# Hybrid decoder layer on one Trainium2 core: the gate and up weights of the SwiGLU as an explicit stream

## The chip, the core and the metric

The kernel runs on one core of one Trainium2 chip. The metric is the device time of one launch in microseconds (us); lower is better. The engines are TensorE (PE, with its weight loads as PEld), VectorE (DVE), ScalarE (ACT), GpSimd (POOL) and SyncE (SP), which issues the DMAs.

## What is computed

One decoder layer on 1,088 tokens (1,024 prompt tokens and 8 x 8 sample tokens): RMSNorm, one input projection, GLA heads and dilated softmax heads, an output projection, then the feed-forward part and a last RMSNorm. The change touches the feed-forward part and what stands next to it:

```python
# D_MODEL = 1024, D_FF = 2816, all float32
h = x + mix                                   # mix = concat(heads) @ w_out
hn = rmsnorm(h, g_ffn)
y = h + (jax.nn.silu(hn @ w_fg) * (hn @ w_fu)) @ w_fd
...
y_prompt = rmsnorm(yp, g_final)
y_sample = rmsnorm(ys, g_final)
```

## The kernel before

Float32 products are made of three matmuls each: every operand is split into `hi` (an ACT copy, L172) and `lo` (a DVE subtraction, L173), and `hi*hi`, `hi*lo` and `lo*hi` are summed in PSUM. `split` is that helper; its two instructions have the lines L172 and L173 whichever tile they serve (`whi`/`wlo` for gate and up weights, `wdhi`/`wdlo` for down's, `ghi`/`glo` for the activated block, `xhi`/`xlo` for the tokens).

The feed-forward part takes the tokens in two halves of 544 (`hf` 0 and 1), and the 2,816 inner features in 11 pairs of 128-wide blocks: 22 calls of `gate_up` in all, numbered 0 to 21 here. A call makes gate and up of its two blocks by the seven products of a Strassen-Winograd scheme (`ORDER`: M1, M6, M5, M7, M2, M3, M4), each 24 matmuls of 272 columns, into PSUM banks `a`, `b` (two of them) and `c`. Each product needs one 128x1024 weight block: A11, A12 and A22 as loaded, S1 to S4 as sums of blocks. POOL makes the four sums (L1095). Blocks and sums take the rooms of a ring of seven (`raw`, 512 KB each). After the products, `after` (L1186 to L1192) combines them into a block `B`: PSUM adds `u`, `v`, `s` on DVE, Silu on ACT, the multiplication on POOL or DVE. `plain` splits `B` into `ghi` and `glo`, and in the next call `down` multiplies that by two blocks of w_down: 8 row tiles `k` with 12 matmuls each into banks a, b, c, b (`ps_d`), each added to the residual `h` by DVE (L1240). A call therefore holds 7 x 24 + 8 x 12 = 264 matmuls.

A scheduler sets the order on each engine by readiness and priority. Loads and sums of a call have a priority offset of 700, the splits of weight blocks 350; nothing else ties them to a place:

```python
with tc.high_priority(offset=700):
    parts = blocks(src, w)
...
with tc.high_priority(offset=350):
    hi, lo = (view(part) for part in parts(block))
```

`load_down` brings two blocks of w_down through two rooms of the same ring `raw`. `final_rows` (called five times in call 11, the first of the second half) finishes the first half's rows in a tile `y` whose tag `wraw` has one room, and sends them out; `h[1]`, 2 MB, is loaded there too. Before the loops, `out_half` makes the output projection of each half: for the second half each of the 16 row tiles is also squared on ACT (L1050 and L1053) and summed on POOL (L1054). `factors(1)` turns that sum into the RMSNorm factors; before, it stands in call 0. `norm_half(1)` uses them in call 10.

Of the kernel before, what the change touches and what calls it, by code (L numbers as in the profile page):

```python
# [11 lines left out]
F32 = mybir.dt.float32  # L12
# [91 lines left out]
def hymba_layer(  # L104
# [926 lines left out]
    def out_half(hf):  # L1031
        os = [load_rows(2 * NH * hf + NH * n) for n in range(2)]
        sq_acc = (ffp if hf else outp).tile([P, 2 * NH], F32, name=f"acc{hf}")
        for f in range(KT):
            if f % 2 == 0:
                ws = load_w_out(f, 1)
            for n in range(2):
# [11 lines left out]
                if f == 0:  # L1049
# [34 lines left out]
    def blocks(src, w):  # L1084

        raw = {}
        turn = [0]

        def room(name):
            t = raw[name] = ffp.tile([P, KT * P], F32, tag="raw", name="raw", bufs=7)[:, :w]  # L1090
            return t

        for name, m, k in (("A11", 0, 0), ("A21", 1, 0), ("A22", 1, 1), ("A12", 0, 1)):
            src(room(name), m, k)
        add = lambda out, a, b, op: pool.tensor_tensor(out=out, in0=raw[a], in1=raw[b], op=op)  # L1095
        add(room("S1"), "A21", "A22", ALU.add)
        add(raw["A21"], "A11", "A21", ALU.subtract)
        raw["S3"] = raw["A21"]
        add(room("S2"), "S1", "A11", ALU.subtract)

        def parts(name):
            if name == "S4":
                add(raw["S2"], "A12", "S2", ALU.subtract)
                raw["S4"] = raw["S2"]
            pair = []
            for part in ("whi", "wlo"):
                if wturn[0] % 3 < 2:
# [3 lines left out]
                pair.append(t[:, :w])  # L1111
            wturn[0] += 1
            split(*pair, raw[name])
            return pair

        return parts

    wturn = [0]

    def winograd(src, w, view, x, nk, after):  # L1120
        with tc.high_priority(offset=700):
            parts = blocks(src, w)
        banks = {"a": psum2.tile([P, 2, 512], F32, tag="a", name="ps_a", bufs=1)[:, :, :NH]}
        for name, block, slot, bk, first in ORDER:
            with tc.high_priority(offset=350):
                hi, lo = (view(part) for part in parts(block))
            if bk not in banks:
                banks[bk] = psum2.tile([P, 2, 512], F32, tag=bk, name=f"ps_{bk}", bufs=2 if bk == "b" else 1)[:, :, :NH]
            for s in range(2):
                for k in range(nk):  # L1130
                    xhi, xlo = x(k, slot)
                    one = lambda l, r, i: mm(out=banks[bk][:, s], lhsT=l[:, k, s], rhs=r, start=first and k == 0 and i == 0,  # L1132
                                             stop=k == nk - 1 and i == 2, skip_group_check=not first)
                    one(hi, xhi, 0)
                    one(hi, xlo, 1)
                    one(lo, xhi, 2)
            with tc.high_priority():
                after(name, banks)
# [35 lines left out]
    def gate_up(i, xs):  # L1174
        s1, u2, v5 = temps()
        B = new_block()

        def src(t, m, k):
            cols = slice((2 * i + m) * P, (2 * i + m + 1) * P)
            t = t.rearrange("p (s k c) -> p s k c", s=2, c=P)  # L1180
            for s, wt in enumerate((w_fg, w_fu)):
                dma(out=t[:, s], in_=wt[:, cols].rearrange("(k two p) c -> two p k c", two=2, p=P)[k])

        def made(slot, c, eng):

            act(out=B[:, slot], in_=c[:, 0], func=AF.Silu)  # L1186
            eng.tensor_tensor(out=B[:, slot], in0=B[:, slot], in1=c[:, 1], op=ALU.mult)

        def after(name, ps):
# [3 lines left out]
            elif name == "M6":  # L1193
                add(u2, s1, "b")
            elif name == "M5":
                add(v5, s1, "c")
            elif name == "M7":
                add(v5, v5, "b")
                made(2, v5, pool)
            elif name == "M2":  # L1200
# [73 lines left out]
    for hf in range(2):  # L1274
        for i in range(NF // 2):
# [5 lines left out]
            if hf == 0 and i == NF // 2 - 1:  # L1281
                xs = norm_half(1)
# [105 lines left out]
```

## Time and profile before

| | |
|---|---|
| median of 3 runs | 1657.88 us (1654.70 to 1661.11) |
| the profiled execution: its own time | 1659.34 us |
| its span in the profile | 1657.6 us |
| mean granted clock of TensorE | 0.952 |
| busy, share of the span: PE / DVE / ACT / POOL | 91% / 60% / 36% / 34% |
| feed-forward part within the span | 781.9 to 1657.6 us |

A share is an average over the whole span, in which the projection, the heads and the feed-forward part have different limits. The feed-forward part takes 876 us, and PE is busy 784 us of these; the rows further down take it apart. The name of a row gives line, engine, operation and tiles (out <- in).

### The profile page before, as it was taken

Reading aid. Unit: us, or ns where it says so; the run is one execution under the profiler, and the core shown is the slowest. Engines: PE = TensorE matmul, PEld = TensorE weight load, DVE = VectorE, ACT = ScalarE, POOL = GpSimd, SP = SyncE. Lnnn points to the kernel's source line nnn. Section 1 sums busy time; section 2 is a strip of 40 time slices with the busy share of each in tenths; the row PEclk is TensorE's granted clock in tenths of the full one; section 3 lists DMA queues with packets and bytes.
Section 4 is the critical chain, followed back from the end, with each engine's and each line's share of the span. In section 5 each row is a group of like instructions: output and inputs, shape, how many; then the busy total and the mean of one; then the engine's idle time right before and its main releaser. Section 6 shows DMA issues by size and latency. Waiting matters only on the chain.

```text
span 1657.6 us, 32292 instructions
## 1 busy us (share of the span) xinstructions
PE 1503.7 (91%) x13363; PEld 1349.4 (81%) x13363; DVE 993.9 (60%) x1673; ACT 590.3 (36%) x1014; POOL 556.1 (34%) x419
## 2 busy tenths in 40 slices
PE   7979999999999998986799999999896999999995
PEld 6867777877777756776799999899886999999995
DVE  5495665632333252346876666766885777666665
ACT  3243332153433453233433333333343333333322
POOL 1493332131121000046633444333542433334411
PEclk9988999999999999988799999999997999999997
DMA  4311021263535366575323222222333322332201
GB/s 148 101 68 35 16 72 37 77 184 106 147 93 143 93 206 182 170 229 168 92 86 101 82 77 90 84 82 85 115 109 131 93 90 77 106 98 78 79 24 54
DMA packets 236659, 170.36 MB, mean 103 GB/s; under 512 B 17728, under 2 KB 223968, under 8 KB 236512
## 3 DMA queue, kind: packets, MB, share of 16 engines
q1 hardware_dynamic: 232304, 168.08, 33.9%
q8 instruction: 105, 1.72, 0.4%
q10 hardware_dynamic: 4208, 0.21, 0.2%
q14 instruction: 42, 0.34, 0.1%
HBM read 142.56 MB, written 25.69 MB: 102 GB/s over the span
## 4 chain that ended last, share of the span: by engine, by line
PE 52%; DVE 18%; POOL 11%; DMA 9%; ACT 4%; issue 4%; SPq 1%; POOLq 0%; ACTq 0%; DVEq 0%
POOL raw L1095 8%; PE ps_mm L201 6%; PE ps_mm L203 6%; PE ps_mm L202 6%; DVE wlo L173 6%; PE ps_b L1132 4%; PE ps_c L1132 3%; PE ps_a L1132 3%; PE ps_d L201 3%; PE ps_d L202 3%; PE ps_d L203 3%; ACT whi L172 3%; DVE glo L173 3%; PE ps_S L840 2%; DMA raw<-in_w_ffn_up_dram 2%
## 5 line engine op out<-in xcount | busy, mean ns | idle before, releaser
L1095 POOL TENSOR_TENSOR raw<-raw 128x1024 f32<-128x1024 f32 x88 | 232.8, 2655 | 518.9 <-DVE wlo L173 336.2
L173 DVE TENSOR_TENSOR wlo<-raw,whi 128x1024 fp32r<-128x1024 f32 x154 | 230.8, 1500 | 104.1 <-ACT whi L172 103.9
L201 PE MATMUL ps_d<-ghi,wdhi 128*128 128x272 f32 (+2 forms) x704 | 214.2, 305 | 41.2 <-DVE h L1240 37.0
L172 ACT ACTIVATE whi<-raw 128x1024 fp32r<-128x1024 f32 x154 | 162.9, 1058 | 210.8 <-issue 80.5
L203 PE MATMUL ps_d<-ghi,wdlo 128*128 128x272 f32 (+2 forms) x704 | 211.0, 301 | 0.9 <-DVE wdlo L173 0.9
L202 PE MATMUL ps_d<-glo,wdhi 128*128 128x272 f32 (+2 forms) x704 | 211.7, 301 | 0.0
L201 PE MATMUL ps_mm<-xhi,whi 128*128 128x384 f32 (+1 forms) x576 | 199.3, 346 | 2.0 <-ACT whi L172 1.6
L203 PE MATMUL ps_mm<-xhi,wlo 128*128 128x384 f32 (+1 forms) x576 | 195.0, 340 | 0.6 <-DVE wlo L173 0.6
L202 PE MATMUL ps_mm<-xlo,whi 128*128 128x384 f32 (+1 forms) x576 | 194.9, 339 | 0.2 <-DVE xlo L278 0.2
L201 PEld LDWEIGHTS ps_d<-ghi,wdhi 128*128 128x128 f32 x704 | 141.4, 201 | 46.3 <-DVE h L1240 41.4
L1132 PE MATMUL ps_b<-xhi,whi 128*128 128x272 f32 x528 | 154.8, 293 | 19.3 <-ACT y L1266 11.3
L1132 PE MATMUL ps_b<-xhi,wlo 128*128 128x272 f32 x528 | 154.1, 292 | 0.8 <-DVE wlo L173 0.8
L1132 PE MATMUL ps_b<-xlo,whi 128*128 128x272 f32 x528 | 153.9, 291 | 0.8 <-DVE xlo L173 0.8
L1240 DVE TENSOR_TENSOR h<-h,ps_d 128x544 f32<-128x544 f32 x168 | 115.6, 712 | 51.4 <-PE ps_d L203 51.1
L203 PEld LDWEIGHTS ps_d<-ghi,wdlo 128*128 128x128 f32 x704 | 141.2, 201 | 1.2 <-DVE wdlo L173 1.2
L202 PEld LDWEIGHTS ps_d<-glo,wdhi 128*128 128x128 f32 x704 | 141.8, 201 | 0.0
L201 PEld LDWEIGHTS ps_mm<-xhi,whi 128*128 128x128 f32 x576 | 110.6, 192 | 12.2 <-issue 7.3
L1132 PEld LDWEIGHTS ps_b<-xhi,whi 128*128 128x128 f32 x528 | 100.9, 191 | 20.6 <-ACT y L1266 11.6
L202 PEld LDWEIGHTS ps_mm<-xlo,whi 128*128 128x128 f32 x576 | 110.5, 192 | 6.7 <-issue 5.7
L203 PEld LDWEIGHTS ps_mm<-xhi,wlo 128*128 128x128 f32 x576 | 110.1, 191 | 7.1 <-issue 5.3
L1132 PE MATMUL ps_a<-xhi,whi 128*128 128x272 f32 x352 | 102.8, 292 | 9.7 <-DVE xa L1046 9.2
L1132 PE MATMUL ps_c<-xhi,wlo 128*128 128x272 f32 x352 | 104.3, 296 | 3.4 <-DVE wlo L173 3.3
(362 smaller groups left out, 3463.2 us busy)
## 6 DMA issues: line engine op xcount, KB each, us to landing
raw<-in_w_ffn_gate_dram SPq DMA_DIRECT2D x88, 256.0 KB, 3.6
raw<-in_w_ffn_up_dram SPq DMA_DIRECT2D x88, 256.0 KB, 4.4
raw<-in_w_ffn_down_dram SPq DMA_DIRECT2D x44, 512.0 KB, 3.4
wraw<-in_w_in_dram SPq DMA_DIRECT2D x22, 512.0 KB, 3.7
raw<-in_cache_swa_k_dram SPq DMA_DIRECT2D x32, 256.0 KB, 4.7
raw<-in_cache_swa_v_dram SPq DMA_DIRECT2D x32, 256.0 KB, 3.6
wraw<-in_w_out_dram SPq DMA_DIRECT2D x12, 512.0 KB, 3.8
xa<-x_dram SPq DMA_DIRECT2D x32, 136.0 KB, 2.4
```

The source lines that it names most:

```text
L172: a = by.tensor_copy(out=hi, in_=raw) if by else act(out=hi, in_=raw, func=AF.Copy)
L173: return a, vec.tensor_tensor(out=lo, in0=raw, in1=hi.bitcast(F32), op=ALU.subtract)
L201: mm(out=ps, lhsT=whi[k], rhs=xhi[k], start=first and k == 0, stop=False)
L202: mm(out=ps, lhsT=whi[k], rhs=xlo[k], start=False, stop=False)
L203: mm(out=ps, lhsT=wlo[k], rhs=xhi[k], start=False, stop=last and k == n - 1)
L840: ins = mm(out=out, lhsT=qres[own, qi * P + 32 * r : qi * P + 32 * r + 32], rhs=rhs, start=True, stop=True)
L1095: add = lambda out, a, b, op: pool.tensor_tensor(out=out, in0=raw[a], in1=raw[b], op=op)
L1132: one = lambda l, r, i: mm(out=banks[bk][:, s], lhsT=l[:, k, s], rhs=r, start=first and k == 0 and i == 0, stop=k == nk - 1 and i == 2, sk ...
L1240: vec.tensor_tensor(out=hk, in0=hk, in1=ps, op=ALU.add)
```

## The change

1. `gate_up_weights(i)` replaces `blocks` and the priorities. It has four parts: `load`, `sums(step)`, `parts(behind)` and the list `made` of split pairs. Product j of a call prepares the weight block of product j + 2: its split is queued behind the instruction that combines product j (`after_all` ties the order with `issue_after`). The last two products prepare the first two blocks of the following call. The following call's loads are issued at j = 0, its S1 and S3 are summed at j = 2 and its S2 at j = 3; a call's own S4 is summed at its j = 0.
2. w_down's two blocks come through the tag `wraw` with its one room, and are loaded and split at j = 0 and j = 1 of the next `gate_up`, behind that product's combining instruction. The last pair of each half is loaded and split directly before its `down`.
3. `plain` is called inside `down`, behind the `h` add of k = 5.
4. The second half's squares leave `out_half`. Calls 1 to 4 load two of the eight row tiles each from x_dram (557 KB), square them with one ACT instruction and add them up on POOL (eight operations of 544 columns). `factors(1)` moves from call 0 to call 5.

```diff
@@ out_half
-        sq_acc = (ffp if hf else outp).tile([P, 2 * NH], F32, name=f"acc{hf}")
+        sq_acc = outp.tile([P, 2 * NH], F32, name="acc") if hf == 0 else None
...
-                if f == 0:
+                if hf:
+                    pass
+                elif f == 0:
                     act(out=sq_acc[:, cs], in_=row, func=AF.Square)
@@ blocks and winograd
-    def blocks(src, w):
...
+    def gate_up_weights(i):
...
+        def load():
+            cols = lambda m: slice((2 * i + m) * P, (2 * i + m + 1) * P)
+            for name, m, k in (("A11", 0, 0), ("A21", 1, 0), ("A22", 1, 1), ("A12", 0, 1)):
+                t = room(name).rearrange("p (s k c) -> p s k c", s=2, c=P)
+                for s, wt in enumerate((w_fg, w_fu)):
+                    dma(out=t[:, s], in_=wt[:, cols(m)].rearrange("(k two p) c -> two p k c", two=2, p=P)[k])
...
+        def sums(step):
+            if step == 0:
+                add(room("S1"), "A21", "A22", ALU.add)
+                add(raw["A21"], "A11", "A21", ALU.subtract)
+                raw["S3"] = raw["A21"]
+            elif step == 1:
+                add(room("S2"), "S1", "A11", ALU.subtract)
+            else:
                 add(raw["S2"], "A12", "S2", ALU.subtract)
                 raw["S4"] = raw["S2"]
+
+        def parts(behind):
+            name = ORDER[len(made)][1]
...
+            with after_all(behind), tc.high_priority(offset=60):
+                split(*pair, raw[name])
+            made.append([t.rearrange("p (s k c) -> p k s c", s=2, c=P) for t in pair])
+
+        return load, sums, parts, made
+
+    @contextmanager
+    def after_all(behind):
+        with ExitStack() as stack:
+            for ins in behind:
+                stack.enter_context(tc.issue_after(ins.ins))
+            yield
@@ gate_up
-    def gate_up(i, xs):
+    def gate_up(xs, own, following, wd):
...
+            with tc.high_priority():
+                ins = after(name, banks)
+            if ins is not None:
+                behind = [ins]
+            if j == 0:
+                own[1](2)
+            if j < 2 and wd is not None:
+                wd(j, behind)
+            if following and j == 0:
+                following[0]()
+            if following and j in (2, 3):
+                following[1](j - 2)
+            if j + 2 < len(ORDER):
+                own[2](behind)
+            elif following:
+                following[2](behind)
         return B
@@ load_down
-        for f in (2 * i, 2 * i + 1):
-            with tc.high_priority(offset=350):
-                raw = ffp.tile([P, KT * P], F32, tag="raw", name="raw", bufs=7)
-                dma(out=raw, in_=w_fd[f * P : (f + 1) * P, :])
-                ws.append([bh.tile([P, D], F32R, tag=f"wd{part}", name=f"wd{part}", bufs=3) for part in ("hi", "lo")])
+
+        def load(j, behind):
+            f = 2 * i + j
+            raw = wpool.tile([P, KT, P], F32, tag="wraw", name="wd_raw", bufs=1).rearrange("p k c -> p (k c)")
+            dma(out=raw, in_=w_fd[f * P : (f + 1) * P, :])
+            ws.append([bh.tile([P, D], F32R, tag=f"wd{part}", name=f"wd{part}", bufs=3) for part in ("hi", "lo")])
+            with after_all(behind):
                 split(*ws[-1], raw)
-        return ws
+
+        return ws, load
@@ down
             with tc.high_priority():
-                vec.tensor_tensor(out=hk, in0=hk, in1=ps, op=ALU.add)
+                ins = vec.tensor_tensor(out=hk, in0=hk, in1=ps, op=ALU.add)
+            if then and k == 5:
+                with after_all([ins]):
+                    then()
@@ the calls
+    calls = [(hf, i) for hf in range(2) for i in range(NF // 2)]
+    own = gate_up_weights(0)
+    own[0]()
+    for step in range(2):
+        own[1](step)
+    for _ in range(2):
+        own[2]([])
+    ready, ws, load = [], None, None
+    sums = ffp.tile([P, 2 * NH], F32, name="acc1")
+    for call, (hf, i) in enumerate(calls):
+        following = gate_up_weights(calls[call + 1][1]) if call + 1 < len(calls) else None
+        B = gate_up(xs, own, following, load)
+        own = following
+        if call in (1, 2, 3, 4):
+
+            t = ffp.tile([P, 4, NH], F32, tag="T", name="T", bufs=1).rearrange("p (k n) t -> p k (n t)", k=2)
+            dma(out=t, in_=x_dram[:, 2 * call - 2 : 2 * call, 2 * NH :])
+            act(out=t, in_=t, func=AF.Square)
+            for k in range(2):
+                if call == 1 and k == 0:
+                    pool.tensor_copy(out=sums, in_=t[:, 0])
+                else:
+                    pool.tensor_tensor(out=sums, in0=sums, in1=t[:, k], op=ALU.add)
+        if call == 5:
+            ps = psum2.tile([P, 2, 512], F32, tag="b", name="ps_f", bufs=2)
+            factors(1, sums, psum2.tile([P, 2, 512], F32, tag="b", name="ps_f", bufs=2)[:, 0], [ps[:, 0], ps[:, 1]])
...
+        if ready:
+            down(ws, ready.pop(), h[hf], lambda: ready.append(plain(B)))
+        else:
+            ready.append(plain(B))
+        ws, load = load_down(i)
+        if (hf, i) == (0, NF // 2 - 1):
+            for j in range(2):
+                load(j, [])
+            down(ws, ready.pop(), h[0])
+            load = None
...
+    for j in range(2):
+        load(j, [])
+    whole, wd = ready.pop(), ws
```

The `hi`/`lo` splits, the sums and DVE's adds then stand otherwise. Three places, as they stand in the two programs:

VectorE (DVE) within one call of the first half, before. `v`, `u` and `s` are the PSUM adds that combine M7, M3 and M4; every `wlo` is the second half of a weight split, every `h` an add of a `down` row tile:

```order
L1190 TENSOR_TENSOR v_11756<-v_11756,ps_b 128x544
L173 TENSOR_TENSOR wlo<-raw,whi 128x1024 x2
L1187 TENSOR_TENSOR B<-B,ps_a 128x272
L1190 TENSOR_TENSOR u_11755<-u_11755,ps_c 128x544
L173 TENSOR_TENSOR wlo<-raw,whi 128x1024
L1190 TENSOR_TENSOR s_11754<-s_11754,ps_b 128x544
L173 TENSOR_TENSOR glo<-B,ghi 128x544
L173 TENSOR_TENSOR wlo<-raw,whi 128x1024
L1240 TENSOR_TENSOR h<-h,ps_d 128x544 x3
L173 TENSOR_TENSOR glo<-B,ghi 128x544
L1240 TENSOR_TENSOR h<-h,ps_d 128x544 x5
```

The same stretch of a call after the change, from the split of M3's block on (the split of M4's block is the `wlo` behind `B`, the next two are M1's and M6's of the next call):

```order
L173 TENSOR_TENSOR wlo<-raw,whi 128x1024
L1266 TENSOR_TENSOR h<-h,ps_d 128x544
L173 TENSOR_TENSOR wdlo<-wd_raw,wdhi 128x1024
L1181 TENSOR_TENSOR B<-B,ps_a 128x272
L173 TENSOR_TENSOR wlo<-raw,whi 128x1024
L1184 TENSOR_TENSOR u_11379<-u_11379,ps_c 128x544
L173 TENSOR_TENSOR wlo<-raw,whi 128x1024
L1184 TENSOR_TENSOR s_11378<-s_11378,ps_b 128x544
L173 TENSOR_TENSOR wlo<-raw,whi 128x1024
L1266 TENSOR_TENSOR h<-h,ps_d 128x544
L173 TENSOR_TENSOR wlo<-raw,whi 128x1024
L1266 TENSOR_TENSOR h<-h,ps_d 128x544 x3
```

Before, one `glo` and one `wlo` stood between `s` and the first three `h`; now a single `wlo` stands there, both `glo` come behind the three `h` (the row after the last one shown), and w_down's second split stands right behind M3's weight split.

GpSimd (POOL), a little over one call of the first half, before (`raw` are the sums of weight blocks, `B` the multiplications):

```order
L1095 TENSOR_TENSOR raw<-raw 128x1024
L1187 TENSOR_TENSOR B<-B,v_11026 128x272
L1095 TENSOR_TENSOR raw<-raw 128x1024 x2
L1187 TENSOR_TENSOR B<-B,u_11025 128x272
L1095 TENSOR_TENSOR raw<-raw 128x1024
L1187 TENSOR_TENSOR B<-B,s_11024 128x272
L1095 TENSOR_TENSOR raw<-raw 128x1024
```

The same queue after the change:

```order
L1104 TENSOR_TENSOR raw<-raw 128x1024 x4
L1181 TENSOR_TENSOR B<-B,v_11380 128x272
L1181 TENSOR_TENSOR B<-B,u_11379 128x272
L1181 TENSOR_TENSOR B<-B,s_11378 128x272
L1104 TENSOR_TENSOR raw<-raw 128x1024 x4
```

The four sums were spread over the call with multiplications between them; now all four stand in a row, ahead of the three multiplications.

SyncE (SP) in call 11 and 12, where the first half's finished rows `y` leave (`out_0_dram`) and w_down's blocks are loaded, with the numbers of the buffers, before:

```order
L1293 DMA h_13423<-x_dram_58 128x8x544
L1271 DMA out_0_dram<-y_13338 128x1024
L1271 DMA out_0_dram<-y_13367 128x1024
L1271 DMA out_0_dram<-y_13396 32x1024
L1218 DMA raw_14143<-in_w_ffn_down_dram 128x1024
L1218 DMA raw_14149<-in_w_ffn_down_dram 128x1024
L1182 DMA raw_14159<-in_w_ffn_gate_dram 128x4x128
L1182 DMA raw_14159<-in_w_ffn_up_dram 128x4x128
```

And after the change, from the last `y` on:

```order
L1300 DMA out_0_dram<-y_13385 32x1024
L1242 DMA wd_raw_13445<-in_w_ffn_down_dram 128x1024
L1102 DMA raw_13822<-in_w_ffn_gate_dram 128x4x128
L1102 DMA raw_13822<-in_w_ffn_up_dram 128x4x128
L1242 DMA wd_raw_13493<-in_w_ffn_down_dram 128x1024
L1242 DMA wd_raw_13810<-in_w_ffn_down_dram 128x1024
L1242 DMA wd_raw_13858<-in_w_ffn_down_dram 128x1024
```

Before, w_down's loads went to rooms of the ring. Now the four stand in one room, `wd_raw`, which is the room of `y` too: the first waits until the last `y` has left, and each of the others until the one ahead of it has been split.

## Rows read from the trace of the kernel before

**Rows 1.** Windows: stretch, length, busy of PE PEld DVE ACT POOL, clock, DMA share, GB/s.
```profile
781.88:863.48 81.60, 66.78 (x448) 64.39 (x449) 61.12 (x70) 31.11 (x40) 47.73 (x30) 0.82 0.30 90
863.48:1155.69 292.21, 276.44 (x2114) 274.69 (x2113) 201.04 (x200) 100.03 (x129) 113.22 (x56) 0.96 0.30 87
1155.69:1333.66 177.97, 149.25 (x1099) 145.27 (x1097) 138.82 (x186) 67.19 (x88) 74.30 (x44) 0.93 0.35 109
1333.66:1587.01 253.35, 240.05 (x1850) 238.53 (x1849) 174.76 (x175) 87.52 (x113) 99.45 (x50) 0.97 0.30 88
```

**Rows 2.** The chain of waits within one call: start, duration, engine, tile, line.
```profile
1370.65 3.00 PE ps_a L1132 x24
...
1382.04 2.35 POOL raw L1095
...
1386.12 5.76 POOL raw L1095 x2
...
1391.90 1.07 ACT whi L172
...
1392.99 1.23 DVE wlo L173
1394.22 0.63 DVE s L1190
1394.85 2.43 DVE glo L173
1397.27 1.70 DVE wlo L173
```

**Rows 3.** Waits, 1333 to 1587: who waited for whom, total, times, longest.
```profile
PE ps_d L201 <- DVE h L1240: 13.3, 7, 1.9
```

**Rows 4.** Windows of one call at full clock and one not, then 3.3 us each.
```profile
1370.49:1405.82 35.33, 33.40 (x267) 33.18 (x265) 25.01 (x25) 12.50 (x17) 14.17 (x7) 1.00 0.31 90
1405.82:1442.67 36.85, 34.94 (x266) 34.72 (x265) 25.03 (x25) 12.51 (x17) 14.16 (x7) 0.95 0.29 86
...
1435.96:1439.30 3.34, 3.34 (x17) 3.34 (x17) 2.24 (x4) 0.00 (x0) 0.00 (x0) 0.52 0.32 125
1399.67:1403.00 3.33, 3.33 (x26) 3.33 (x27) 3.10 (x6) 0.00 (x0) 0.00 (x0) 1.00 0.49 157
```

**Rows 5.** Timeline of PE around a short wait.
```profile
1327.90 0.39 PE L201 MATMUL ps_d<-ghi,wdhi 128*128 128x272 f32 x1 [0.45 <-DVE h L1240]
...
1328.26 0.28 PE L203 MATMUL ps_d<-ghi,wdlo 128*128 128x272 f32 x1
```

**Rows 6.** Timeline of DVE in the call of rows 2.
```profile
1387.10 2.50 DVE L173 TENSOR_TENSOR wlo<-raw,whi 128x1024 fp32r<-128x1024 f32 x1 [1.57 <-ACT whi L172]
```

**Rows 7.** The sums on POOL, 1330 to 1590: duration in ns, min/median/max.
```profile
L1095 POOL TENSOR_TENSOR raw<-raw x28: 2385/2397/3392, 1345.2 to 1575.5; 128x1024 f32<-128x1024 f32 x28
```

**Rows 8.** The second half's sums of squares, and who waited for them.
```profile
L1054 POOL TENSOR_TENSOR acc<-acc,sq x28: 757/776/1639, 723.8 to 788.6; 128x272 f32<-128x272 f32 x28
...
PE ps_f L1063: 3.8, 1
```

**Rows 9.** Small DVE operations, 1200 to 1300: duration in ns, min/median/max.
```profile
L156 DVE TENSOR_TENSOR st<-st x15: 151/159/2309, 1221.5 to 1285.8; 128x1 f32<-128x1 f32 x15
```

**Rows 10.** Timeline of SP: the last three issues of `y` to leave, from first to last.
```profile
1257.57 30.51 SPq L1271 DMA_DIRECT2D out_dram<-y  x3
```

**Rows 11.** Timeline of PE and ACT there.
```profile
1289.21 0.59 PE L201 MATMUL ps_d<-ghi,wdhi 128*128 128x272 f32 x1 [3.00 <-DVE st L1258]
...
1275.64 1.02 ACT L1266 ACTIVATE y<-ps_y 32x1024 f32<-32x1024 f32 x1 [0.55 <-DMA out_dram<-y]
```

**Rows 12.** Landing times in us: loads (page, median) and `y` (min/median/max).
```profile
raw<-in_w_ffn_up_dram SPq DMA_DIRECT2D x88, 256.0 KB, 4.4
raw<-in_w_ffn_down_dram SPq DMA_DIRECT2D x44, 512.0 KB, 3.4
...
DMA to landing us min/median/max: 1.9/2.6/9.5
```

More of the change, by code (lines that the diff above doesn't have):

```diff
@@ L1110, in parts @@
                     t = bh.tile([P, KT * P], F32R, tag=part, name=part, bufs=1)
[L1111 to L1124, printed above, removed]
-            with tc.high_priority(offset=350):
[L1126 to L1138, printed above, removed]
+                pair.append(t)
+            turn[0] += 1
+            with after_all(behind), tc.high_priority(offset=60):
[8 more added lines that the diff above has]
+            yield
     def temps():
@@ L1193, in after @@
             elif name == "M6":
[L1194 removed]
+                return add(u2, s1, "b")
             elif name == "M5":
[L1196 removed]
+                return add(v5, s1, "c")
             elif name == "M7":
[L1198 removed]
+                ins = add(v5, v5, "b")
                 made(2, v5, pool)
+                return ins
             elif name == "M2":
[L1201 removed]
+                return made(0, ps["a"], vec)
             elif name == "M3":
[L1203 removed]
+                ins = add(u2, u2, "c")
                 made(3, u2, pool)
+                return ins
             else:
[L1206 removed]
+                ins = add(s1, s1, "b")
                 made(1, s1, pool)
[L1209 to L1210 removed]
+                return ins
+        banks, behind = {}, []
+        n = KT // 2
+        for j, (name, _, slot, bk, first) in enumerate(ORDER):
+            if bk not in banks:
+                banks[bk] = psum2.tile([P, 2, 512], F32, tag=bk, name=f"ps_{bk}", bufs=2 if bk == "b" else 1)[:, :, :NH]
+            hi, lo = own[3][j]
+            for s in range(2):
+                for k in range(n):
+                    xhi, xlo = (part[:, slot] for part in xs[k])
+                    for a, (l, r) in enumerate(((hi, xhi), (hi, xlo), (lo, xhi))):
+                        mm(out=banks[bk][:, s], lhsT=l[:, k, s], rhs=r, start=first and k == 0 and a == 0,
+                           stop=k == n - 1 and a == 2, skip_group_check=not first)
+            with tc.high_priority():
[14 more added lines that the diff above has]
+                following[2](behind)
         return B
@@ L1228, in plain, with down @@
         return hi, lo
-    def down(ws, g, h):
+    def down(ws, g, h, then=None):
         for k in range(KT):
@@ L1244, in hymba_layer @@
     xs = norm_half(0)
[L1245 removed]
+    out_half(1)
     outp.release()
```

61 lines of the change are left out of this document (13 added, 48 removed).

## The prediction, made before the changed kernel ran

> **What bounds the kernel now.** I read the windows first [rows 1]. The feed-forward part falls into a start of two calls (81.60 us), eight regular calls (292.21), four calls around the change of halves (177.97), seven regular calls (253.35) and a tail. A regular call takes (292.21 + 253.35) / 15 = 36.37 us. PE is busy in 94.6% of these stretches and its clock is granted at 0.96 to 0.97, so PE sets their pace, and the question is what its other 5% are. The chain of waits gives the floor: 24 matmuls in 3.00 us [rows 2], 0.125 us each, and 264 x 0.125 = 33.0 us, with edges 33.1. So a call loses 3.3 us.
>
> The waits say where: PE waits once a call, before a row tile of `down`, for an `h` add: 13.3 us in 7 calls, 1.9 each [rows 3]. The windows by call show the other part: 35.33 us at a clock of 1.00, but 36.85 at 0.95 [rows 4]. Two of three calls go like the second. There the stretch behind the wait runs at 0.52, that is at the 1.2 GHz level instead of 2.4, with 17 matmuls in 3.34 us where the other call does 26; that costs 36.85 - 35.33 = 1.5 us. A wait of 0.45 us has no such sequel: the first matmul behind it is slow, two take 0.36 us instead of 0.25 [rows 5].
>
> The chain says why the `h` add is late [rows 2]. POOL makes S1, S3 and S2 late (1382.04, 1386.12), since a room of the ring came free late; S2's and S4's splits slide behind them; `s` ends at 1394.85, and then `glo` (2.43) and `wlo` (1.70) stand in DVE's queue before the first of three `h` adds. PE needs the banks these adds free, and restarts when the first is done.
>
> **The change, part by part.** *Regular calls, removed.* The order rows show that `glo` and its neighbour leave the place between `s` and the three `h`; one `wlo` is left there. 4.1 us of queue become 1.23, so the wait of 1.9 and its sequel of 1.5 go: at most 3.3 us a call.
>
> *Regular calls, added.* POOL's four sums now stand in a row and meet the splits of M3, of w_down and of M4. The chain and the timeline of DVE show what a meeting does [rows 2, 6]: the two sums from 1386.12 take 5.76 us in place of 2 x 2.40 [rows 7], and a `wlo` that starts at 1387.10 takes 2.50 in place of 1.23. The split waited for the sum that was running, went next, and the second sum waited for it. They take turns, whole instruction by whole instruction. The Trainium skill ("SBUF — State Buffer", section "Who interferes with whom") says that a VectorE instruction with two SBUF inputs and a GpSimd instruction that reads SBUF exclude each other, that the one issued first goes, and that the other blocks fully; the rows agree. Were they independent, the sum below would be 11 us lower.
>
> By hand, with 0 at M6's first matmul. PE has M6, M1, M5, M7, M2 and M3, 2 of M4 and 33 of `down` before it needs M4's low part: 179 x 0.125 = 22.4. M6 is done after 48, at 6.0; its add takes 0.63 and M7's `wlo` 1.23, to 7.9. M7's block is S3, made in A21's room, and the ring hands that room to the next call's A22; its up half lands 4.4 later [rows 12], at 12.3. S1 runs to 14.7. M3's `wlo` is queued behind the add of M7 (done at 13.5), so it waits to 14.7 and ends at 15.9 (wanted at 17.0). S3 then runs to 18.3, `wdlo` to 19.5, S2 to 21.9, M4's `wlo` to 23.1. That is 0.7 us late, a short wait like that one [rows 5]. The number of loads is the same but for four, and the DMA engines are 30% busy [rows 1], so their order on SP costs nothing in itself. What else stands in the queues has slack: the multiplications behind the four sums feed `glo`, which is now needed a whole call later. So a call takes 33.1 + 0.6 = 33.7. Bounds: 33.1 (S1 starts outside that second) and 36.4 (the rival below). The gain is 36.37 - 33.7 = 2.7, for the 15 regular calls and for one more in the tail, which begins with the same kind of call: 16 x 2.7 = **-43 us**.
>
> *The start.* The 14 POOL sums of the second half's squares go (0.78 each [rows 8]); one PE wait for them, 3.8 us, goes too. For it, calls 1 to 4 get eight POOL operations of 544 columns. Between 0.78 for 272 and 2.40 for 1024 columns that is some 1.4 us each, an estimate, or 11 us in all, which can hold up a split each time; their four ACT squares and four loads lie beside other work. Bounds -4 and +11; I take **+4**, because the first two calls now also make two calls' splits in a fixed order.
>
> *factors(1) in call 5.* Some 15 small DVE operations enter the queue between the products' adds. Such an operation takes 0.16, but up to 2.31 when a POOL operation holds it up [rows 9]. Eight of them stand ahead of M2's multiplication, which frees bank a: 8 x 0.16 = 1.3 at least, 8 x 2.3 = 18 at most. With ten small PE instructions and one stretch at half clock (1.5) I take **+5**, near the lower end, since the median is 0.16; for the range 0 to +10.
>
> *The change of halves.* The single room `wraw` now serves `y` and all of w_down's loads. Before, the last `y` is issued by 1257.57 + 30.51 = 1288.1 [rows 10], and `down` starts at 1289.21 [rows 11] with weights already there. After: `y` lands 2.6 later, the first load takes 3.4 [rows 12], its split 1.07 + 1.23, the second load and split the same: 1288.1 + 2.6 + 5.7 + 5.7 = 1302.1. PE has 16 matmuls (2.0 us) that need the first block alone, so it waits 12.9 - 2.0 = 10.9, in two pieces. The 1.5 us of half clock behind it stands against a like one before (its wait of 3.00). I take **+11**. Below, 0, if the rows leave earlier than before (the last PE transposes for `y`, 1275.64 on ACT, may come forward); above, +25, if `y` lands in 9.5 [rows 12] and both pieces cost clock.
>
> Sum: -43 + 4 + 5 + 11 = -23 against the profiled execution's own 1659.3, which lies 1.5 above the median of the runs: **1636 us**.
>
> **The rivals.** *A, slower: the turns fall the wrong way.* All hangs on when A22 lands. At 13.4 instead of 12.3, S1 runs to 15.8, M3's `wlo` to 17.0, S3 to 19.4, `wdlo` to 20.6, S2 to 23.0 and M4's `wlo` to 24.2: 1.8 us late. That is as long as the wait removed, so the half clock comes with it: 33.1 + 1.8 + 1.5 = 36.4, nothing gained in any call, and start, factors and boundary are lost: 1659 + 20 = **1679**. It decides from about 1 us of lateness. For it: only one second lies between the cases, and POOL sums of 3.39 occur [rows 7]. Against: landing later than 13.5 lets the split go first, and no wait is left.
>
> *B, no change: the single room and the start cost their upper bounds.* -43 + 11 + 5 + 25 = -2: **1657**; half of that excess gives 1648. For it: the loads of call 12 and call 13 queue in the same room, and landing times of 9.5 stand in the trace. Against: only five `y` tiles pass.
>
> *C, faster: no late split and a cheap boundary.* 16 x 3.3 = -53, start 0, factors +4, boundary +5: **1615**. For it: A22 may land just outside the second. Against: two pieces of it must go well together.
>
> That the change does not do what it says can be left out: the order rows show the splits and sums where the text puts them.
>
> **How the numbers follow.** A run tells no change from change at about 0.5%, 8 us. Likeliest case 0.62 (its own range 1625 to 1648), A 0.11, B 0.14, C 0.13. Faster: 0.62 + 0.13 = 0.75; same: B, 0.14; slower: A, 0.11. The range from 1614 to 1656 takes in C and nearly all of B and leaves A out.
>
> **What would show it.** Right: regular calls of 33.1 to 34.3 us; the 1.9 us wait for `h` gone; a short wait on PE for `wlo` before M4's low part; the granted clock near 1.00 in these windows; around the change of halves a PE wait for `wdlo` or `wdhi` of some 11 us that was not there. Wrong: calls still near 36 with PE waiting for `wlo` (A); regular calls good but the four boundary calls over 195 us (B). If the regular calls are good and the total is still at 1658, the boundary and the start were sized wrong, not the mechanism.

## The result and the profile after

The changed kernel takes 1630.31 us (median of 4 runs, 1627.30 to 1631.03), the kernel before 1656.29 (4 runs). The ratio is 0.9835 with a 95% interval of 0.9809 to 0.9861: 1.65% faster. The span of the profiled execution is 1629.0 us.

The windows of the changed kernel, cut at the same places of the program as those of before [rows 1] and finer (length, busy time of PE, PEld, DVE, ACT and POOL, granted clock, DMA share, GB/s): the two first calls, calls 2 to 4, 5 and 6, 7 to 9, the four calls around the change of halves, the seven regular calls behind it, the tail.

```profile
779.21:858.71 79.50, 67.29 (x454) 64.47 (x455) 56.01 (x53) 34.12 (x41) 54.17 (x31) 0.88 0.41 118
858.71:958.56 99.85, 99.85 (x794) 99.58 (x793) 74.48 (x75) 37.78 (x48) 49.31 (x21) 1.00 0.32 96
958.56:1033.25 74.69, 70.65 (x544) 69.56 (x543) 56.11 (x67) 25.22 (x32) 30.09 (x14) 0.98 0.29 85
1033.25:1133.12 99.87, 99.87 (x795) 99.70 (x794) 74.42 (x75) 37.77 (x48) 49.35 (x21) 1.00 0.33 96
1133.12:1327.91 194.79, 153.43 (x1097) 147.92 (x1096) 137.04 (x186) 68.35 (x87) 74.18 (x44) 0.89 0.32 100
1327.91:1560.86 232.95, 232.95 (x1851) 232.44 (x1850) 173.65 (x175) 88.14 (x112) 115.50 (x50) 1.00 0.30 89
1560.86:1629.00 68.14, 49.07 (x393) 48.42 (x391) 37.36 (x81) 19.16 (x30) 9.36 (x10) 0.87 0.14 49
```

In the regular calls PE is busy for the whole window and its clock is granted at 1.00: 232.95 / 7 = 33.28 us a call. No wait is left in them to remove. Against before, the feed-forward part is 875.7 - 849.8 = 25.9 us shorter, about the change of the median (the two profiled executions differ by 28.6; the rest lies ahead of this part). It is made of -46.3 in 15 regular calls (15 x (36.37 - 33.28)), +8.1 in calls 5 and 6 (74.69 against 2 x 33.28), +16.8 at the change of halves (194.79 against 177.97), -2.1 in the two first calls and -2.5 in the tail.

The wait for `h` of 1.9 us per call [rows 3] is gone; in the list of waits of the seven calls no wait of PE stands at all. How close it is can be read from one call. Timeline of DVE, then POOL, then PE, of the changed kernel (start, duration, line, what is written and read):

```profile
1043.84 0.72 DVE L1184 TENSOR_TENSOR v<-v,ps_b 128x544 f32<-128x544 f32 x1 [1.10 <-PE ps_b L1216]
1044.48 1.89 DVE L173 TENSOR_TENSOR wlo<-raw,whi 128x1024 fp32r<-128x1024 f32 x1
1046.29 0.71 DVE L1266 TENSOR_TENSOR h<-h,ps_d 128x544 f32<-128x544 f32 x1
1046.92 2.81 DVE L173 TENSOR_TENSOR wdlo<-wd_raw,wdhi 128x1024 fp32r<-128x1024 f32 x1
1049.65 0.42 DVE L1181 TENSOR_TENSOR B<-B,ps_a 128x272 f32<-128x272 f32 x1
1050.00 3.06 DVE L173 TENSOR_TENSOR wlo<-raw,whi 128x1024 fp32r<-128x1024 f32 x1
...
1042.88 9.11 POOL L1104 TENSOR_TENSOR raw<-raw 128x1024 f32<-128x1024 f32 x3 [14.23 <-DVE wlo L173]
...
1053.07 0.29 PE L201 MATMUL ps_d<-ghi,wdhi 128*128 128x272 f32 x1
1053.19 0.32 PE L1216 MATMUL ps_b<-xhi,wlo 128*128 128x272 f32 x1
```

Three splits (1.22 us each when alone) take 1.89, 2.81 and 3.06, and three sums (2.40 each) take 9.11 instead of 7.2. M4's split ends at 1050.00 + 3.06 = 1053.06 and PE's first matmul that reads it starts at 1053.19, with no wait in front of it.

What starts this row of sums is not what the prediction names. Before its first sum, S1, POOL waits 14.23 us for a DVE `wlo`. It is the split of M2's block, the last reader of the room that S1 takes. M6's first matmul, the zero of the walk, and the chain on ACT, DVE and SP that leads there:

```profile
1030.73 0.29 PE L1216 MATMUL ps_b<-xhi,whi 128*128 128x272 f32 x1
...
1037.35 0.61 ACT L1186 ACTIVATE s<-ps_a 128x544 f32<-128x544 f32 x1
...
1037.99 0.72 DVE L1184 TENSOR_TENSOR u<-s,ps_b 128x544 f32<-128x544 f32 x1 [6.23 <-ACT s L1186]
1038.62 1.22 DVE L173 TENSOR_TENSOR wlo<-raw,whi 128x1024 fp32r<-128x1024 f32 x1
...
1041.53 1.22 DVE L173 TENSOR_TENSOR wlo<-raw,whi 128x1024 fp32r<-128x1024 f32 x1
...
1026.82 0.51 SPq L1102 DMA_DIRECT2D raw<-in_w_ffn_up_dram  x1
...
1039.92 0.37 SPq L1102 DMA_DIRECT2D raw<-in_w_ffn_gate_dram  x1
```

M7's split is the `wlo` at 1038.62, M2's the one at 1041.53, and S1 starts at 1042.88. By the order of the program's loads, the one at 1026.82 is A22's up half; it lands 3.2 us later, at 1030.03, some 13 us before S1 starts. The load that follows M7's split, at 1039.92, is A12's.

At the change of halves PE now waits for w_down's splits. Timelines of PE and of ACT there, with the idle time ahead of an instruction and what ended it:

```profile
1273.97 0.59 PE L201 MATMUL ps_d<-ghi,wdhi 128*128 128x272 f32 x1 [6.73 <-ACT wdhi L172]
1279.78 0.39 PE L201 MATMUL ps_d<-ghi,wdhi 128*128 128x272 f32 x1 [2.72 <-ACT wdhi L172]
...
1272.86 1.06 ACT L172 ACTIVATE wdhi<-wd_raw 128x1024 fp32r<-128x1024 f32 x1 [1.28 <-DMA wd_raw<-in_w_ffn_down_dram]
1278.67 1.06 ACT L172 ACTIVATE wdhi<-wd_raw 128x1024 fp32r<-128x1024 f32 x1 [4.75 <-DMA wd_raw<-in_w_ffn_down_dram]
```

Before, PE's only wait at this `down` was one of 3.00 for `st` [rows 11].

### The profile page after: what moved, and what is told of

Read it like the earlier page. It is cut to its first block, busy times and chain, and to the rows that moved or that the text cites. A ratio compares the mean times of both kernels' runs of the same rounds, so it can differ in the third digit from the quotient of the medians.

```text
span 1629.0 us, 32149 instructions
## 1 busy us (share of the span) xinstructions
PE 1490.5 (92%) x13363; PEld 1338.2 (82%) x13363; DVE 987.9 (61%) x1673; ACT 590.3 (36%) x1002; POOL 584.1 (36%) x413
## 4 chain that ended last, share of the span: by engine, by line
PE 71%; DVE 12%; DMA 9%; ACT 2%; POOL 2%; issue 2%; SPq 1%; ACTq 0%; DVEq 0%; POOLq 0%
PE ps_b L1216 11%; PE ps_a L1216 6%; PE ps_c L1216 6%; PE ps_mm L201 6%; PE ps_mm L203 6%; PE ps_mm L202 6%; PE ps_d L201 5%; PE ps_d L203 5%; PE ps_d L202 5%; PE ps_S L840 2%; DMA x_dram<-xa 2%; DVE wlo L173 2%; PE ps_X L982 1%; PE ps_T L938 1%; DMA out_dram<-y 1%
## 5 line engine op out<-in xcount | busy, mean ns | idle before, releaser
L1104 POOL TENSOR_TENSOR raw<-raw 128x1024 f32<-128x1024 f32 x88 | 260.1, 2964 | 433.7 <-DVE wlo L173 280.1
L173 DVE TENSOR_TENSOR wlo<-raw,whi 128x1024 fp32r<-128x1024 f32 x154 | 242.2, 1575 | 0.0
L201 PE MATMUL ps_d<-ghi,wdhi 128*128 128x272 f32 (+2 forms) x704 | 205.5, 294 | 16.3 <-ACT wdhi L172 9.4
L202 PE MATMUL ps_d<-glo,wdhi 128*128 128x272 f32 (+2 forms) x704 | 205.6, 293 | 1.1 <-DVE glo L173 1.1
L203 PE MATMUL ps_d<-ghi,wdlo 128*128 128x272 f32 (+2 forms) x704 | 201.2, 292 | 0.0
L1216 PE MATMUL ps_b<-xhi,wlo 128*128 128x272 f32 x528 | 158.1, 299 | 5.6 <-DVE wlo L173 5.6
L201 PEld LDWEIGHTS ps_d<-ghi,wdhi 128*128 128x128 f32 x704 | 135.1, 192 | 18.2 <-ACT wdhi L172 11.6
L202 PEld LDWEIGHTS ps_d<-glo,wdhi 128*128 128x128 f32 x704 | 135.8, 193 | 1.5 <-DVE glo L173 1.5
L203 PEld LDWEIGHTS ps_d<-ghi,wdlo 128*128 128x128 f32 x704 | 133.4, 192 | 0.0
L201 PEld LDWEIGHTS ps_mm<-xhi,whi 128*128 128x128 f32 x576 | 110.7, 192 | 12.2 <-issue 7.3
L1216 PEld LDWEIGHTS ps_b<-xhi,wlo 128*128 128x128 f32 x528 | 103.3, 196 | 7.9 <-DVE wlo L173 6.9
```

The source lines that it names most:

```text
L173: return a, vec.tensor_tensor(out=lo, in0=raw, in1=hi.bitcast(F32), op=ALU.subtract)
L201: mm(out=ps, lhsT=whi[k], rhs=xhi[k], start=first and k == 0, stop=False)
L202: mm(out=ps, lhsT=whi[k], rhs=xlo[k], start=False, stop=False)
L203: mm(out=ps, lhsT=wlo[k], rhs=xhi[k], start=False, stop=last and k == n - 1)
```

## The experiments

All times are medians; the ratio is that to the kernel before, with its 95% interval.

### One line of the change, alone and taken out

e1 is the kernel before with `plain` queued behind k = 5, and nothing else:

```diff
...
-            before, g = g, plain(B)
...
-            if before:
-                down(ws, before, h[hf])
+            if g:
+                made = []
+                down(ws, g, h[hf], lambda: made.append(plain(B)))
+                g = made.pop()
+            else:
+                g = plain(B)
```

> The kernel before with one thing of the change: plain (ghi and glo) is queued behind the h add of k = 5 of down. Sums, splits and rooms stay as before. Theory A (the order of glo in DVE's queue is the whole regular gain): the 1.9 us wait for h falls to 0.9 or less, since only one wlo is left ahead of the first h, the half-clock stretch behind it goes, regular calls take 33.3 to 34.3 us in place of 36.4, and the total is 1610 to 1627. Rival B (the gain comes from POOL's sums starting earlier, which splits and s follow): s and that wlo stay as late as before, a wait of 1 us or more remains, regular calls take 35 us or more, and the total is above 1635.

It takes 1623.30 us, ratio 0.9792 (0.9770 to 0.9814): one change of order, and it is faster than the whole change, by 0.4% with intervals that just touch. Its windows (calls 2 to 9, change of halves, calls 14 to 20):

```profile
858.65:1132.22 273.57, 267.41 (x2115) 265.67 (x2113) 196.06 (x200) 100.06 (x129) 117.24 (x56) 1.00 0.32 93
1132.22:1312.29 180.07, 149.86 (x1098) 145.81 (x1097) 138.40 (x186) 67.77 (x88) 76.53 (x44) 0.92 0.35 108
1312.29:1551.19 238.90, 233.99 (x1850) 232.47 (x1849) 170.62 (x176) 87.56 (x113) 102.97 (x50) 1.00 0.31 93
```

PE's only row among the waits of the last of these (total, times, longest):

```profile
PE ps_d L201 <- DVE h L1247: 4.9, 7, 0.7
```

238.90 / 7 = 34.13 us a call. The wait fell from 1.9 to 0.7 us, and with it the half clock went: the granted clock is 1.00. So 1.2 us of wait and the 1.0 us that the half clock cost on average (1.5 in two of three calls) went together.

e2 is the changed kernel with `plain` ahead of `down` again:

```diff
...
-        if ready:
-            down(ws, ready.pop(), h[hf], lambda: ready.append(plain(B)))
-        else:
-            ready.append(plain(B))
+        ready.append(plain(B))
+        if len(ready) > 1:
+            down(ws, ready.pop(0), h[hf])
```

> The changed kernel without its third part: plain is called before down again, so one glo stands among the h adds of k = 0 to 4 and the other ahead of s. Theory A (glo's place): waits for h of 1 us or more come back in most calls, regular calls take 34.5 us or more, total 1650 or more. Rival B (the earlier sums): with s earlier there is room for glo; regular calls stay at 33.3 to 33.8 us, total 1630 to 1640.

It takes 1631.82 us, ratio 0.9848 (0.9823 to 0.9872), like the changed kernel, and calls 14 to 20 read:

```profile
1326.49:1558.62 232.13, 232.13 (x1851) 232.13 (x1850) 173.24 (x175) 88.48 (x112) 115.98 (x50) 1.00 0.30 89
```

The two runs together say that the wait had two cures, each sufficient for most of it: to queue `plain` later (e1), or to have the rest of the change, with the stream (e2). In e2 one `glo` stands ahead of `s`, as it did not before, and finds DVE idle:

```profile
1448.97 0.73 DVE L173 TENSOR_TENSOR glo<-B,ghi 128x544 fp32r<-128x544 f32 x1 [1.35 <-ACT ghi L172]
1449.61 0.71 DVE L1184 TENSOR_TENSOR s<-s,ps_b 128x544 f32<-128x544 f32 x1
```

So in both runs a single `wlo`, and no `glo`, stands between `s` and the first `h` add; earlier sums with `glo` left in that place were not run. Theory A of e1 held, and so did rival B of e2. The prediction ascribed the gain to `glo` and a neighbour leaving this place, which fits both runs. But the third part of the change, which moves `plain`, is not needed for it: with the stream in place that part is worth nothing.

### Does a split wait for one sum, or for all?

e7 makes S1 twice in each call:

```diff
                 add(room("S1"), "A21", "A22", ALU.add)
+                add(raw["S1"], "A21", "A22", ALU.add)
```

> The changed kernel with the sum S1 made twice in every call, 2.4 us more of POOL ahead of S3 and S2 with the same result; DVE's order stays. Theory A (splits and sums take turns, one sum per split, so that more sums in the row don't make a split later): M4's split ends as before within 0.5 us, regular calls take 33.2 to 33.8 us, total 1628 to 1640. Rival B (a split waits out the sums queued ahead of it): M4's split is 2.4 us or more late, regular calls take 35.5 us or more, total 1665 or more.

It takes 1653.45 us, ratio 0.9974 (0.9954 to 0.9994); seven calls take 240.71 us, 34.39 each. Neither total was right, but the timelines of POOL and DVE tell the theories apart:

```profile
1053.71 5.74 POOL L1104 TENSOR_TENSOR raw<-raw 128x1024 f32<-128x1024 f32 x2 [13.48 <-DVE wlo L173]
1059.40 1.76 POOL L1182 TENSOR_TENSOR B<-B,v 128x272 f32<-128x272 f32 x1
1061.12 6.70 POOL L1104 TENSOR_TENSOR raw<-raw 128x1024 f32<-128x1024 f32 x2
...
1060.80 1.44 DVE L173 TENSOR_TENSOR wlo<-raw,whi 128x1024 fp32r<-128x1024 f32 x1
...
1068.95 1.23 DVE L173 TENSOR_TENSOR wlo<-raw,whi 128x1024 fp32r<-128x1024 f32 x1 [1.25 <-ACT whi L172]
```

M4's split ends at 1062.24, 18.2 us behind M1's start at 1044.08, where the changed kernel has it at 19.8, and PE reads it at 1064.02: it is earlier, not later, although the call holds 2.4 us more of sums. That alone does not decide, since the multiplication of `v` now runs behind the second sum and the split met it, which is shorter, in place of a sum. M3's split decides:

```profile
1055.31 1.87 DVE L173 TENSOR_TENSOR wlo<-raw,whi 128x1024 fp32r<-128x1024 f32 x1
```

It ends at 1057.18, 3.5 us behind the start of S1 at 1053.71. In the changed kernel it ends at 1046.37, also 3.5 behind S1's start, with one sum fewer still queued behind that one. Splits and POOL instructions take turns, one for one; theory A's mechanism holds. What the theory overlooked is the end of the row: S2, now last and later, is the block of the next call's M6, whose split stands in DVE's queue ahead of the first `h` adds (1068.95). So PE waits for `h`, as its waits over two calls say:

```profile
PE ps_d L201 <- DVE h L1267: 1.2, 2, 0.7
```

The length of POOL's row decides over the `h` adds, then, and only its turns over M4's split.

e4 writes the low half of M4's split twice, directly one behind the other:

```diff
-                split(*pair, raw[name])
+                done = split(*pair, raw[name])
+                if name == "A22":
+                    with after_all(done[1:]):
+                        vec.tensor_tensor(out=pair[1], in0=raw[name], in1=pair[0].bitcast(F32), op=ALU.subtract)
```

> The changed kernel with the low half of M4's weight split written twice in every call, one extra DVE instruction of 1.22 us whose result is the same, directly behind the first. In the changed kernel that split ends 0.1 us before PE wants it by the trace. Theory A (the margin is that thin, and this split is the critical one): PE waits for it 1.0 to 1.9 us in every call; if half clock follows, regular calls take 35.8 to 36.7 us and the total is 1670 or more, if not, 34.3 to 35.2 and 1647 to 1662. Rival B (the margin is larger than the trace makes it look): regular calls stay below 33.8 us, total below 1640.

It takes 1645.93 us, ratio 0.9924 (0.9900 to 0.9947); seven calls take 236.92 us, 33.85 each, at a clock of 1.00. This is between the theories, and a reason lies in the edit: the scheduler answered it by placing other matmuls on PE ahead of M4 (24 of `down` where 21 stood), so that 1.2 us more of DVE work met a later need. PE still waits for the second writing in five of the seven calls, 0.2 us at most. So the split is close to PE's need, but how thin the margin of the changed kernel is stays unmeasured.

### The price of the single room

e3 gives w_down's raw blocks a room of their own. The space comes from g_final's row copy, which moves into the factor tile once that is read:

```diff
-            raw = wpool.tile([P, KT, P], F32, tag="wraw", name="wd_raw", bufs=1).rearrange("p k c -> p (k c)")
+            raw = fin.tile([P, KT, P], F32, tag="wdraw", name="wd_raw", bufs=1).rearrange("p k c -> p (k c)")
...
-    gfin = fin.tile([P, D], F32, name="gfin")
-    dma(out=gfin, in_=g_final.partition_broadcast(P))
...
             xs = norm_half(1)
+            gfin = rstd_bc[:, :D]
+            dma(out=gfin, in_=g_final.partition_broadcast(P))
```

> The changed kernel with a room of its own for w_down's raw blocks (g_final's row copy moves into the factor tile, which is free by then). Theory A (the single room is what the change of halves costs): the PE waits for wdhi there, 6.73 and 2.72 us, go with the half-clock stretches behind them; the four calls around the change of halves take 194.8 - 9.5 - 3 = 182 us, the total is 1616 to 1621, regular calls stay at 33.3. Rival B (the loss sits in y's own chain: one room, its way out, the small DVE operations): the waits move to y or st, the four calls stay above 190 us, total 1626 or more.

It takes 1611.69 us, ratio 0.9723 (0.9701 to 0.9745), and the four calls take

```profile
1131.46:1307.04 175.58, 146.72 (x1099) 142.08 (x1098) 136.21 (x186) 68.58 (x87) 80.01 (x44) 0.93 0.36 114
```

175.58 against 194.79: the shared room cost 19.2 us, more than the two PE waits of 9.45 and two stretches at half clock. PE is idle for 28.9 us where it was for 41.4, and busy for 146.7 where it was for 153.4 with the same matmuls, at a clock of 0.93 where it was 0.89. Both waits for `wdhi` are gone. Theory A, with a larger size.

### The price of the fourth part

e5 undoes it:

```diff
...
-                if hf:
-                    pass
-                elif f == 0:
+                if f == 0:
...
-    out_half(1)
+    sums = out_half(1)
...
-        if call in (1, 2, 3, 4):
+        if call in ():
...
-        if call == 5:
+        if call == 0:
```

> The changed kernel without its fourth part: the second half's squares are made in out_half again and factors(1) stands in call 0. Theory A (the squares leaving out_half give the start its gain, and factors in call 5 costs 8.1 us in calls 5 and 6, which take 74.69 in place of 2 x 33.28): calls 5 and 6 fall to 66.6 us, the first matmul of the feed-forward part starts 2 to 3 us later and the two first calls take 2 us more; total 1625 to 1628. Rival B (the start's gain is the stream's): calls 5 and 6 fall and the start keeps its time, total 1621 to 1623.

It takes 1622.86 us, ratio 0.9785 (0.9769 to 0.9802). Calls 5 and 6, and the two first calls' end, read

```profile
856.61:956.48 99.87, 99.87 (x795) 99.59 (x794) 74.48 (x75) 37.77 (x48) 49.34 (x21) 1.00 0.32 96
956.48:1023.06 66.58, 66.58 (x530) 66.40 (x529) 49.68 (x50) 25.18 (x32) 32.91 (x14) 1.00 0.32 96
```

66.58 against 74.69: the price of `factors(1)` in call 5 is 8.1 us. The start gained nothing from moving the squares: its first call begins at 776.25 and call 2 at 856.61, 80.4 us, where the changed kernel has 79.5; in the profiles of all runs here this stretch takes 79.5 to 81.6. The beginning of the feed-forward part itself lies between 775.9 and 781.9 in the profiles with the squares in place, so a difference of 2 or 3 us there is no finding. Rival B.

e6 keeps the squares where the change put them, but queues `factors(1)` behind the last `h` add of call 5:

```diff
...
+            if last and k == KT - 1:
+                with after_all([ins]):
+                    last()
...
+            def second():
+                ps = psum2.tile([P, 2, 512], F32, tag="b", name="ps_f", bufs=2)
+                factors(1, sums, ps[:, 1, 256:], [ps[:, 0], ps[:, 1]])
...
```

> The changed kernel with factors(1) queued behind the last h add of call 5, where DVE is idle for 6.2 us in every call and POOL makes no sum, in one PSUM tile in place of two. Theory A (its small DVE operations cost because they stand among the splits and sums): calls 5 and 6 fall from 74.69 to 67 to 69 us and the total to 1622 to 1625. Rival B (the cost is that of PE's small instructions and of the bank, wherever they stand): 72 us or more, total above 1627.

It takes 1626.92 us (1620.12 to 1628.90), ratio 0.9800 (0.9775 to 0.9825); calls 5 to 7 take 101.86 us, 2.0 over 3 x 33.28. In the trace that is theory A: 8.1 became 2.0, with one PSUM tile in place of two. The total lies between the two theories' ranges. The same small operation in the timeline of the changed kernel:

```profile
970.87 2.24 DVE L154 TENSOR_SCALAR st<-st 128x5 int32<-128x5 int32 x1
```

And in that of e6:

```profile
987.40 0.17 DVE L154 TENSOR_SCALAR st<-st 128x5 int32<-128x5 int32 x1
```

Among the sums it took 2.24 us, where POOL is idle 0.17.

e8 joins the edits of e3 and e6.

> The changed kernel with the room of its own for w_down (1611.7 alone) and with factors(1) at the end of call 5. Theory A (the two losses are independent): 1611.7 less what the other kernel gains, 1603 to 1606. Rival B (the change of halves absorbs part of it): 1607 to 1612.

1609.07 us, ratio 0.9701 (0.9685 to 0.9717): calls 5 to 7 take 101.88, so e6's gain is there, and 2.7 us of it go at the change of halves:

```profile
1125.42:1303.69 178.27, 149.63 (x1098) 144.97 (x1097) 135.99 (x186) 68.73 (x87) 80.08 (x44) 0.91 0.35 112
```

PE is idle there as long as in e3 (28.6 against 28.9 us) but busy 2.9 longer, at a clock of 0.91 against 0.93; why the clock is lower was not followed. The total is in rival B's range.

### A version that beats both

e9 joins the edits of e3 and e5: the stream, the place of `glo`, an own room, and the fourth part undone.

> The changed kernel with a room of its own for w_down and without its fourth part (squares in out_half, factors(1) in call 0): what is left is the stream and the place of glo. Theory A (the two losses add: 19 us at the change of halves, 8 us in calls 5 and 6): 1601 to 1605. Rival B (factors in call 0 takes its price at the start once the rest is faster): 1607 or more.

1607.87 us, ratio 0.9696 (0.9673 to 0.9719). Calls 2 to 9 are at 33.29 us each, but the change of halves takes 181.76. Neither theory's reason: the start does not pay (80.8 us), the change of halves is 6.2 longer than in e3, and why was not settled. There PE has one long wait, 11.44 us for `y`, which stood in the kernel before as well. e10 gives `y` a second room, and e11 keeps one room but queues h's 2 MB load behind the third `y`:

```diff
...
+        if t0 // P % 2:
+            y = ffp.tile([P, 4, NH], F32, tag="T", name="y", bufs=1).rearrange("p s n -> p (s n)")[:, :D].rearrange("p (f c) -> p f c", f=2)
+        else:
+            y = wpool.tile([P, KT, P], F32, tag="wraw", name="y", bufs=1).rearrange("p (f k) c -> p f (k c)", f=2)
...
-        act(out=sq[:m], in_=y[:m], func=AF.Square, accum_out=st[:m, 0:1])
+        act(out=ps[:m].rearrange("p f c -> p (f c)"), in_=y[:m], func=AF.Square, accum_out=st[:m, 0:1])
```

```diff
...
             h[1] = residual()
-            dma(out=h[1], in_=x_dram[:, :, 2 * NH :])
+            with after_all([third]):
+                dma(out=h[1], in_=x_dram[:, :, 2 * NH :])
```

> The same with two rooms for y in turn (the second is that of T; the squares that nobody reads go to the PSUM bank). Theory A (PE's wait of 11.3 us at the change of halves is for y's one room): that wait falls below 4 us and the total to 1588 to 1595. Rival B (the wait is for the way out of the third y, which lands behind the 2 MB load of h, whatever the rooms): 8 us or more stay, total above 1597.

> The same with one room for y, but the 2 MB load of h queued on SP behind the third y instead of ahead of it. Theory B (the load of h ahead of it makes that y land in 9 us instead of 2.6): PE's wait of 11.3 us falls to 4 to 6 us, total 1594 to 1599. Theory A (the room alone): the wait stays above 9 us, total 1601 or more.

e10 takes 1585.01 us, ratio 0.9554 (0.9530 to 0.9578); e11 1604.54, ratio 0.9673 (0.9654 to 0.9691). PE's timeline at that place, e9 first, then e11 (in e10 no such wait stands), and the windows of e10 (change of halves, regular calls, tail):

```profile
1234.37 0.59 PE L1214 MATMUL ps_b<-xhi,whi 128*128 128x272 f32 x1 [11.44 <-ACT y L1291]
```

```profile
1232.17 0.60 PE L1214 MATMUL ps_b<-xhi,whi 128*128 128x272 f32 x1 [7.21 <-ACT y L1291]
```

```profile
1123.25:1287.30 164.05, 148.45 (x1098) 144.47 (x1096) 135.44 (x186) 67.69 (x87) 74.94 (x44) 0.95 0.39 122
1287.30:1520.31 233.01, 233.01 (x1852) 232.46 (x1850) 173.78 (x175) 88.14 (x112) 115.53 (x50) 1.00 0.30 89
1520.31:1582.40 62.09, 49.62 (x393) 48.66 (x391) 36.07 (x81) 19.04 (x30) 9.30 (x10) 0.90 0.16 54
```

Theory A of e10: the room was the wait, and the four calls get 17.7 us shorter (181.76 to 164.05). The tail, which sends out the last rows through the same rooms, is at 62.09 where the changed kernel has 68.14. In e11 4.2 us of the wait went with the load's place, as the landing times of `y` (min/median/max) of e9, of e11 and, last, of e10 show:

```profile
DMA to landing us min/median/max: 2.6/3.0/6.7
```

```profile
DMA to landing us min/median/max: 2.6/3.0/3.2
```

```profile
DMA to landing us min/median/max: 2.6/3.0/7.8
```

So both were in it, but the room decides: in e10 the slowest `y` lands as late as 7.8 us, and PE does not wait for it.

e12 asks what the stream itself is worth: the kernel before with `glo` moved as in e1 and `y` in two rooms as in e10.

> The kernel before with glo queued behind k = 5 and two rooms for y: everything of the best kernel (1585.0) except the stream of gate and up weights and the room for w_down. Theory A (the stream is worth the 0.85 us a call by which regular calls differ, 34.13 against 33.28, and little else): 17 x 0.85 = 14 us more than the best, 1597 to 1602. Rival B (the stream also carries the start and the change of halves): 1605 or more.

1595.49 us, ratio 0.9624 (0.9587 to 0.9662), 10.5 more than e10. Theory A's mechanism, and 1.5 us under its range: regular calls differ as expected, since those of e12 take 34.13 to 34.26 us, and some of it comes back at the change of halves (160.1 us in e12). e10 also holds w_down's own room, which goes with the stream, since e12 still loads w_down through the ring.

## Why the prediction was right

The forecast was 1636, the result 1630.3, inside the likeliest case's own range. Of the 5.7 us between them 3.0 lie in the base (1659.3 against the median before of 1656.3), the rest in the sum (-23 against -26). The named places of gain and loss were right, but the start of the sums' row in a regular call came out right by luck. Step by step:

- *The regular calls, removed.* Right in size: the wait and its half-clock sequel went. The cause fits as well: no `glo` is left between `s` and the `h` adds. What was not foreseen is that two parts of the change bring this about, each enough for most of it (e1, e2).
- *The regular calls, added: where the row starts.* The walk by hand put S1's start at 12.3, and it stands at 12.2 behind M6's first matmul (1042.88 less 1030.73). The path to it was another. The walk has M7's split done at 7.9, A22's load into that room behind it, and S1 waiting for the landing. In the trace M6's add waits for ACT's copy of M1 and starts at 7.3, not 6.0; M7's split is done at 9.1; the room goes to A12; and A22 had landed before M6 began. S1 waited for M2's split, done at 12.0. Two wrong readings met at the right number. The short wait on PE before M4's low part, named as a sign, did not appear.
- *The regular calls, added: the turns.* That sums and splits exclude each other and alternate was right. M3's split was put at 15.9 and ends at 15.6; M4's at 23.1 and ends at 22.3. The term that was mis-sized is the turn: 2.40 + 1.23 = 3.6 us were counted for a sum and a split, and a turn took 3.3 to 3.4 (M3's split ends at 1046.37, `wdlo` at 1049.73, M4's at 1053.06). Two turns make 0.5 us, and M3's split is 0.3 early; together that is the 0.7 us of lateness that was forecast. So the call is at 33.28 and not 33.7, and 16 calls gave 49 us in place of 43. The Trainium skill's rule ("SBUF — State Buffer", section "Who interferes with whom": a VectorE instruction with two SBUF inputs contends with a GpSimd instruction that reads SBUF, and the lock is exclusive) agrees with the turns of this trace and of e7; the recorded durations of the two instructions overlap by 0.3 us at each turn.
- *The start, +4.* It came out at -2.1, within what the start varies. The bound was taken too much to the dear side: the POOL operations put into calls 2 to 4 delayed nothing (99.85 us, 33.28 each).
- *factors(1) in call 5, +5.* It cost 8.1, in the range of 0 to 10; three of its operations were held up for 2.2 to 2.4 us each, more than "near the lower end" allowed.
- *The change of halves, +11.* PE's two waits came as worked out (9.45 us, against 10.9), in the two pieces named. The total is +16.8, of which 12.6 are more idle time of PE and 4.2 more busy time at a lower clock (0.89 against 0.93). The prediction set the half clock against a like stretch before and so put this second term at nothing. e3 prices the room at 19.2.
- The errors partly cancel: the gain was put 6 us too low in the calls, the start 6 too dear, and the two losses 3 and 6 too cheap.
- *Rival A* was tied to the landing of A22, which lies some 13 us ahead of S1 and decides nothing; by this trace it is M2's split that would have to come about 1 us later, and no run moved it. *Rival B* did not come. Of *rival C* one half came, calls without a late split (33.28), and the other, a cheap boundary, did not.

## What to carry to other kernels

When a wait stands at the end of a queue, try the one-line reorder by itself before rebuilding the stream that feeds it: here the line gave 35 us alone, the rebuilt stream with w_down's own room 10 us more where all else was mended (e12, e10), and the two side edits that came with it cost 19 and 8 us by their own runs (e3, e5). These prices come from different kernels and do not add up to the total. A staging room that two streams share should be counted at the place where both run, not in the steady state: it cost no PE wait in the regular calls and 19 us in the four around the change of halves. And before a small chain of operations is moved, see which engine is idle in the target place: the same chain cost 8 us among POOL's sums and 2 us behind the last add.

## What the runs showed of the hardware

- VectorE splits and GpSimd sums alternate whole instructions (9.11 us for three sums with two splits in between). One sum more in the queue does not hold a waiting split longer (3.5 us from S1's start to the end of M3's split in the changed kernel and in e7), and a turn is 0.3 us shorter than the two durations together.
- A wait of 0.7 us once a call left the granted clock at 1.00 (e1), while the 1.9 us wait of before was followed by half clock in two of three calls [rows 4].
- With h's load of 2 MB queued ahead of the third `y`, the slowest `y` (512 KB) landed in 6.7 us, with the load behind it in 3.2 (e9, e11).
